# A hybrid S5/conformer decoder layer: the S5 scan by round, the out-projection by token tile, joint evacuation of two tiles

## The chip, the cores and the metric

The kernel runs on one core of one Trainium2 chip. The metric is device time in microseconds (us) of one execution, lower is better. Before the change the median of three runs is 2294.46 us (2292.49 to 2294.57).

## What is computed

One inference step of one layer, all in float32: 2048 prompt tokens and 8 further sequences with one token each, model width 1024. Two sub-layers stand one behind the other, each between two RMS norms:

```
h = rmsnorm(x);  p = h @ w_in                       # 1024 -> 512 (u) + 512 (cv) + 512 (cg)
s = S5(u): 32 groups x 64 complex states, a linear recurrence over the tokens;
    y = Re(C h_t) + D u;  a = gelu(y);  s = a * sigmoid(a @ w_glu + b)
c = silu(layernorm(causal depthwise conv, width 31, of cv * sigmoid(cg)))
x = x + rmsnorm(concat(s, c) @ w_out)               # 1024 -> 1024
h = rmsnorm(x);  up = conv3(h @ w_up)               # 1024 -> 2 x 2816
x = x + rmsnorm((silu(up_gate) * up_val) @ w_down)  # 2816 -> 1024
```

The states of the recurrence and of both convolutions are outputs too.

## The kernel before, in words

**Tiles and rounds.** The tokens are cut into six tiles of 344 (the last: 328 and the 8 single tokens), with channels on the partitions (`TILES`, line 24). Two tiles are a round (`ROUNDS`), and `ORDER` (line 32) lists the stages: in(0), in(1), in(2) up to the u columns, out(0), the rest of in(2), ffn(0), out(1), the last down-projection of round 0 as ffn(0,1), ffn(1,0), out(2), ffn(1,1), ffn(2). "in" is the projection by w_in, "out" the GLU and the projection by w_out (`mix_out`, line 2007), "ffn" the up- and down-projections (line 2071).

**Matmuls.** Each operand in float32 is split into a high and a low float32r part, and `group` (line 1105) makes three matmuls for each block of 128 channels: 24 for a 1024-deep product of one tile.

**Weights.** `wl` lists the weight tiles in order of use; each holds up to 128x8x128 values. At its first use a tile is loaded raw (0.52 MB), split by ACT (wh) and VectorE (wlo), and both halves are stored to DRAM (wd); later uses load the two halves, 1.05 MB. There are three raw buffers and three for each half (`NRAW, NW`), and `w_next` (line 872) loads two to three tiles ahead. All these transfers are issued by SyncE (SP).

**PSUM.** The projections rotate through four one-bank tiles `ps` (`ps_tile`, line 613), and results of evacuation through four SBUF buffers of 344 columns (`ev`, line 883).

**S5.** Tokens are cut into chunks of 8. `s5_part` (line 1471) loads u and the matrix Bd into the slot UR (and ST), multiplies, scans over the chunks on VectorE with a doubling scheme (`fma`, levels `lev`), stores the last state (CR), multiplies by Md and Cd and stores the result (ad); `s5_out` (line 1609) loads it back and applies the GELU. Scans are made for round 0 (86 chunks, two parts of 16 groups) and for rounds 1 and 2 together (170 chunks, four parts of 8 groups).

**Convolution.** `conv(r)` (line 1676) runs 31 taps over four channel blocks and two halves on VectorE, then the layer norm. For rounds 1 and 2 the result is stored (cd) and loaded again by `fetch` (cf); `split_c` (line 1768) makes cHL for the out-projection.

**Background work.** S5, conv, the norms after a projection (`mid`, line 1798: RMS norm, residual x from DRAM as xr, store x1d, second norm) and `finish` are generators. They are spawned with a due number, and advanced between matmul groups as long as estimated engine clocks (`clk`) allow. `back(r)` (line 2164) spawns conv(r) and the S5 parts at the start of ffn(r-1).

**Order.** A `Recorder` collects all instructions. `place()` (line 253) simulates the engines with cost formulas, takes among the ready instructions the one with the lowest priority number, and so fixes the order of every engine's queue and the buffer of every tile. `first(n)` (line 202) lowers the number by n. An instruction goes to the chip by one line, L408, so the profile tells the groups apart by tile names.

```
SCANS = [(0,), (1, 2)]
ps_mm = pool("ps_mm", NPS, space=bass.MemoryType.PSUM)      # NPS = 4
for m in range(8):                                          # out-projection
    w_ = w_next()
    for i in ROUNDS[r]:
        ps = ps_tile()
```

Of the kernel before, what the change touches and what calls it, by code (L numbers as in the profile page):

```python
# [19 lines left out]
G = 32  # L20
# [5 lines left out]
CHUNKS = [86, 86, 84]  # L26
SCANS = [(0,), (1, 2)]
S5_LOAD = [2500, 5000]
S5_TURN = [7500, 9000]
PARTS = [4, 4, 4, 4, 6]  # L30
# [5 lines left out]
NPS = 4  # L36
EVM = 4
NRAW, NW = 3, 3
PACE = [1.0, 1.6, 1.6]
# [492 lines left out]
def kernel(  # L532
# [80 lines left out]
    def ps_tile():  # L613
        if len(out_at) >= NPS:
            wait_pe(out_at[-NPS])
        return ps_mm.tile([128, 512], F32, name="ps", tag="mm")

# [88 lines left out]
    def free(n=1):  # L706
        live[0] -= n
# [14 lines left out]
    msk = const.tile([128, 16], F32, name="msk")  # L722
    mi = small.tile([128, 16], I32, name="mi", tag="ev", bufs=EVM)
    nc.gpsimd.iota(mi, pattern=[[1, 16]], base=112, channel_multiplier=-1)
# [20 lines left out]
    h0 = const.tile([128, 2, 16, NS], F32, name="h0")  # L745
    CR = [const.tile([128, 2, 16], F32, name=f"CR{j}") for j in range(2)]
    aS = const.tile([128, 4, NS], F32, name="aS")
# [49 lines left out]
    for what in ORDER:  # L797
        if what[0] == "in":
            for o in IN_ORDER[what[2]:what[3]]:
                wl.append(cols(w_in, 0, 8, o * 128, 128))  # L800
        elif what[0] == "out":
            for o in range(2):
                wl.append(cols(w_glu, 0, 4, o * 256, 256))
            for o in range(8):
                wl.append(cols(w_out, 0, 8, o * 128, 128))
        else:
            for kind, a in ffn_steps[what[1]][what[2]]:
                if kind == "up":
                    wl.append(cols(w_up, 0, 8, a * 128, 128))
                    wl.append(cols(w_up, 0, 8, (NJ + a) * 128, 128))  # L810
                else:
                    for m in range(16 if what[1:] == (2, 1) else 8):
                        m %= 8
                        wl.append(cols(w_down, part_of[a][0], part_of[a][-1] + 1, m * 128, 128))
# [20 lines left out]
    def w_load_to(i):  # L835
        while w_pos[0] <= min(i, len(wl) - 1):
            n = w_pos[0]
            src, sh, key = wl[n]
            if first_use[key] != n:
                hl = halves[n] = w_tiles(n)  # L840
                for k in range(2):
                    nc.sync.dma_start(hl[k].bitcast(F32), staged[first_use[key]][:, k])
                w_pos[0] += 1
                continue
            t = wp.tile([128, 8, 128], F32, name="wraw", tag="raw", bufs=NRAW)
            v = t.rearrange("p a b -> p (a b)")[:, :sh[0] * sh[1]].rearrange("p (a b) -> p a b", a=sh[0])
            nc.sync.dma_start(v, src)
            w_raw[n] = v
            w_pos[0] += 1

    def w_split_to(i):
        while w_pos[1] <= min(i, len(wl) - 1):
            n = w_pos[1]
            if n in halves:
                hl = w_shaped(n, halves.pop(n))
            else:
                raw = w_raw.pop(n)
                flat = w_tiles(n)
                hl = w_shaped(n, flat)
                with nc.first(700 if n > 1 else 0):  # L860
                    act(hl[0], raw)
                    m = hl[0].shape[1] // 2
                    for c in (slice(0, m), slice(m, 2 * m)):
                        tt(hl[1][:, c], raw[:, c], hl[0][:, c].bitcast(F32), OP.subtract)
                if n in staged:
                    for k in range(2):
                        nc.sync.dma_start(staged[n][:, k], flat[k].bitcast(F32))
            w_hl[n] = hl
            w_at[n] = max(clk.values())
            w_pos[1] += 1  # L870
# [12 lines left out]
    def ev(name, shape=None):  # L883

        return view(small.tile([128, EV], F32, name=name, tag="ev", bufs=EVM), shape or [128, EV])

    def bev(name, shape=None):

        return view(small.tile([128, EV], F32, name=name, tag="bev", bufs=8 - EVM), shape or [128, EV])

# [15 lines left out]
    scans = [0]  # L906
    S5_PARTS = [[(0, g) for g in range(0, G, 16)], [(1, g) for g in range(0, G, 8)]]

# [562 lines left out]
    def s5_part(j, g0, ng):  # L1471

        C = sum(CHUNKS[r] for r in SCANS[j])
        last = j == 1
        C8 = C + (NS if last else 0)
        gp = 2 if last else 4
        na = ng // 2
        yield both(flag("mats"), *(flag("u", r) for r in SCANS[j]))
        if last:
            yield flag("carry", 0, g0 // 16 * 16)  # L1480
        if g0 >= 2 * ng:
# [61 lines left out]
        scans[0] += 1  # L1543
        if last:
            fma(R[:, :, :, 0:1], CR[0][:, :, ha].unsqueeze(3), PWr[:, 0, :, ha], PWi[:, 0, :, ha], 1)
            yield None
# [17 lines left out]
        for n in range(2):  # L1564
            for b in range(2):
                o = S[n * 64:(n + 1) * 64, b::2]
                i = slice(b * 64, (b + 1) * 64)
                copy(o[:, :, 1:C], R[i, n, :, 0:C - 1], "act")
                if last:
                    copy(o[:, :, 0], CR[0][i, n, ha], "act")  # L1570
                    copy(o[:, :, C:C8], h0[i, n, ha], "act")
                else:
                    nc.vector.memset(o[:, :, 0], 0.0)
            yield None
# [34 lines left out]
    def s5_out(r):  # L1609

        C = CHUNKS[r]
        last = r == 2
        j = min(r, 1)
        yield both(*(flag("y", *k) for k in S5_PARTS[j]))
        yield can(1)
        t = slot([128, 4, 8, C], F32, f"aR{r}")
        c0 = sum(CHUNKS[SCANS[j][0]:r])
        src = add[j].rearrange("g h t c -> (g h) t c").rearrange("(k p) t c -> p k t c", p=128)
        for k in range(4):
            nc.sync.dma_start(t[:, k], src[:, k, :, c0:c0 + C])  # L1620
        if last:
            nc.sync.dma_start(aS, ads.rearrange("g h c -> (g h) c").rearrange("(k p) c -> p k c", p=128))
        yield after(0)
        tf = t.rearrange("p k t c -> p (k t c)")
        act(tf, tf, AF.Gelu)
        if last:
            act(aS, aS, AF.Gelu)
        aR[r] = t
        flags["a", r] = True
# [46 lines left out]
    def conv(r):  # L1676
# [6 lines left out]
        if r:  # L1683
            yield both(*(flag("y", *k) for k in S5_PARTS[1][:2]))
        yield can(1)
# [182 lines left out]
    def finish_end(i, y, sqs):  # L1868
# [10 lines left out]
        for c in range(3):  # L1879
            xt = XT[c // 2][:m, c % 2]  # L1880
            for b in range(2):
                if n > 3 and n < 6:
                    yt = ps_tr.tile([128, 512], F32, name="trp", tag="tr")
                else:
                    yt = ps_mm.tile([128, 512], F32, name="ps", tag="mm")
                for k in range(4):
# [16 lines left out]
    def out_ssm():  # L1903
        yield both(*(flag("carry", *k) for k in S5_PARTS[1]))
        yield after(6000)
        t, = yield from raw_tiles(1)
        pt = yield from tr_tile()
        for n in range(2):
            tr(pt[:16, n * 128:n * 128 + 128], CR[1][:, n], ident)
            tr(pt[:, 256 + n * 128:384 + n * 128], hS[:, n].rearrange("p s a -> p (s a)"), ident)  # L1910
# [42 lines left out]
    def mix_in(r, x0, x1):  # L1953
# [17 lines left out]
        for oi, n in seq:  # L1971
# [10 lines left out]
            if oi < 4:  # L1982
                us = ev("us", [128, 8, 43])
                act(us[:, :, :cn].rearrange("p s c -> p c s"), ps[:, :np_].rearrange("p (c s) -> p c s", s=8))
                if w > np_:
                    act(uS[:, oi, :], ps[:, np_:w])
                c0 = n * 43 + (CHUNKS[1] if r == 2 else 0)
                nc.sync.dma_start(udd[min(r, 1)][oi * 128:(oi + 1) * 128, :, c0:c0 + cn], us[:, :, :cn])
            elif oi < 8:
# [17 lines left out]
    def mix_out(r):  # L2007
# [37 lines left out]
        for i in ROUNDS[r]:  # L2045
            sqs[i] = small.tile([128, 344], F32, name="msq", tag="msq", bufs=2)
        for m in range(8):
            w_ = w_next()
            for i in ROUNDS[r]:
                w = wid(i)  # L2050
# [7 lines left out]
                tick()  # L2058
        free(4)
        for i in ROUNDS[r]:  # L2060
            spawn(mid(i, mx[i], sqs[i]), 375 + 400 * r)
# [9 lines left out]
    def ffn(r, last):  # L2071
# [9 lines left out]
        for kind, a in ffn_steps[r][last]:  # L2081
            if kind == "up":
# [9 lines left out]
                for hv in range(2):  # L2092
                    w_ = w_next()
                    jj = hv * NJ + j
                    for n, i in enumerate(ROUNDS[r]):
                        t0, np_, ns = TILES[i]
# [4 lines left out]
                              lambda k: hl[1][:, k, 0:w + 2], 8)  # L2101
                        acc = ev("acc")
                        act(acc[:, :w], ps[:, 2:w + 2], AF.Identity, scale=FC[:, jj, 2:3], bias=FC[:, jj, 3:4])
# [60 lines left out]
    def back(r):  # L2164
        spawn(conv(r), 260 + 400 * r, ("dve", "act"), PACE[r])
        if r < 2:
            for n, (j, g0) in enumerate(S5_PARTS[r]):
                spawn(s5_part(j, g0, G // len(S5_PARTS[r])), 190 + n + 400 * r, pace=PACE[r])
        if r == 0:
            spawn(s5_out(r), 192)  # L2170
# [70 lines left out]
```

## Time and profile before

| | |
|---|---|
| median of the runs | 2294.46 us |
| profiled execution | 2296.11 us |
| its span | 2294.3 us |
| TensorE busy | 2186.8 us (95%) |
| VectorE busy | 1540.8 us (67%) |
| ScalarE busy | 867.9 us (38%) |
| GpSimd busy | 103.8 us (5%) |
| DMA | 436.32 MB, mean 190 GB/s |
| mean granted TensorE clock | 0.969 of full speed |

The span runs from the first to the last instruction. PE is TensorE's matmul, PEld its weight load, DVE VectorE, ACT ScalarE, POOL GpSimd, SP SyncE. The granted clock is a share of 2.4 GHz; 0.5 is 1.2 GHz. A group reads "out<-in": the tile written and those read. The DMA share is the mean busy share of the 16 DMA engines, so 1.0 means that all were busy all the time. A wait is put down to the engine and tile that came last.

### The profile page before, as it was taken

The numbers are of one execution on the slowest core, as the hardware profiler recorded it, in microseconds if no ns is written. First come the engines' busy times: TensorE is split into PE (matmuls) and PEld (weight loads), VectorE is DVE, ScalarE is ACT, GpSimd is POOL, SyncE is SP. The second block draws the span as 40 slices with busy tenths as digits, with TensorE's granted clock in tenths as the row PEclk, the third lists the DMA queues.
The fourth block names the chain that finished last, engine by engine and source line by source line (L and its number), as shares of the span: only waits on it lengthen the run. The fifth ranks groups of instructions, "written<-read, shape, count | busy, mean of one in ns | idle before, by whom it ended". The sixth has DMA issues, their size and how long they took to land.

```text
span 2294.3 us, 36725 instructions
## 1 busy us (share of the span) xinstructions
PE 2186.8 (95%) x13923; PEld 2169.6 (95%) x13923; DVE 1540.8 (67%) x3636; ACT 867.9 (38%) x1677; POOL 103.8 (5%) x114
## 2 busy tenths in 40 slices
PE   8998889999999999986899999999998999999998
PEld 8998889999998999976899999999998999999998
DVE  7979865379698999961799995544428624334344
ACT  5665345345543534432443212243225322112134
POOL 1465000000000000000000000000000000000000
PEclk9998789999999999997999999999999999999999
DMA  9999857695858576544654443463546543443546
GB/s 303 273 303 263 193 160 239 165 287 171 256 177 249 165 247 215 179 154 166 218 204 150 157 142 116 153 193 133 193 148 214 178 140 118 165 133 125 186 160 215
DMA packets 267549, 436.32 MB, mean 190 GB/s; under 512 B 60736, under 2 KB 165944, under 8 KB 263733
## 3 DMA queue, kind: packets, MB, share of 16 engines
q1 hardware_dynamic: 266630, 432.62, 59.7%
q8 instruction: 110, 1.80, 0.3%
q0 software_dynamic: 352, 0.67, 0.1%
q10 hardware_dynamic: 391, 0.69, 0.1%
q14 instruction: 66, 0.54, 0.1%
HBM read 293.02 MB, written 140.37 MB: 189 GB/s over the span
## 4 chain that ended last, share of the span: by engine, by line
PE 84%; DVE 9%; DMA 3%; ACT 2%; issue 1%; SPq 1%; POOL 0%; DVEq 0%; ACTq 0%; POOLq 0%
PE ps L408 79%; PE trp L408 4%; DVE acc L408 3%; DVE ST L408 1%; DVE UR L408 1%; DVE wlo L408 1%; DVE mx L408 1%; DMA UR<-ud 1%; DVE st L408 1%; DMA xa<-in_x_prompt_dram 1%; SPq L408 1%; DVE sqs L408 1%; DMA ST<-Bd 0%; ACT UR L408 0%; DVE c L408 0%
## 5 line engine op out<-in xcount | busy, mean ns | idle before, releaser
L408 PE MATMUL ps<-h,wh 128*128 128x346 f32 (+3 forms) x5376 | 1295.2, 323 | 16.1 <-ACT us L408 7.7
L408 PEld LDWEIGHTS ps<-h,wh 128*128 128x128 f32 x5376 | 937.6, 190 | 18.1 <-ACT us L408 7.8
L408 PE MATMUL ps<-h,wlo 128*128 128x346 f32 (+3 forms) x2688 | 866.2, 322 | 0.4 <-DMA wlo<-wd 0.4
L408 PE MATMUL ps<-f,wh 128*128 128x344 f32 (+1 forms) x2112 | 503.6, 322 | 8.8 <-DVE y L408 8.8
L408 PEld LDWEIGHTS ps<-h,wlo 128*128 128x128 f32 x2688 | 510.0, 190 | 0.8 <-DMA wlo<-wd 0.7
L408 DVE SCALAR_TENSOR_TENSOR acc<-ps,FC,acc 128x344 f32<-128x344 f32 (+1 forms) x528 | 302.1, 573 | 266.9 <-ACT acc L408 191.7
L408 PEld LDWEIGHTS ps<-f,wh 128*128 128x128 f32 x2112 | 366.1, 189 | 9.2 <-DVE y L408 9.0
L408 DVE SCALAR_TENSOR_TENSOR acc<-c,V,acc 128x344 f32<-128x344 f32 (+1 forms) x609 | 350.3, 575 | 10.6
L408 PE MATMUL ps<-f,wlo 128*128 128x344 f32 (+1 forms) x1056 | 338.9, 321 | 0.0
L408 ACT ACTIVATE acc<-ps,FC 128x344 f32<-128x344 f32 (+1 forms) x264 | 167.5, 635 | 367.1 <-PE ps L408 366.2
L408 PEld LDWEIGHTS ps<-f,wlo 128*128 128x128 f32 x1056 | 199.6, 189 | 0.0
L408 DVE TENSOR_TENSOR y<-y,ps 128x344 f32<-128x344 f32 (+1 forms) x192 | 97.1, 508 | 115.1 <-PE ps L408 114.8
L408 DVE TENSOR_TENSOR wlo<-wraw,wh 128x512 fp32r<-128x512 f32 (+2 forms) x212 | 122.6, 620 | 45.2 <-ACT wh L408 44.5
L408 ACT ACTIVATE f<-acc 128x344 fp32r<-128x344 f32 (+1 forms) x132 | 64.8, 491 | 224.1 <-DVE acc L408 223.8
L408 ACT ACTIVATE wh<-wraw 128x1024 fp32r<-128x1024 f32 (+2 forms) x106 | 96.5, 912 | 94.5 <-PE ps L408 66.4
L408 ACT ACTIVATE acc<-acc 128x344 f32<-128x344 f32 (+1 forms) x132 | 64.8, 491 | 171.3 <-DVE acc L408 169.8
L408 DVE TENSOR_TENSOR msq<-msq,sq 128x344 f32<-128x344 f32 (+1 forms) x84 | 42.9, 514 | 115.2 <-ACT sq L408 115.1
L408 PE MATMUL ps<-cHL,wh 128*128 128x344 f32 (+1 forms) x384 | 94.2, 328 | 18.5 <-ACT cHL L408 18.1
L408 PE MATMUL ps<-sHL,wh 128*128 128x344 f32 (+1 forms) x384 | 92.7, 324 | 0.0
L408 DVE TENSOR_TENSOR f<-acc,f 128x344 fp32r<-128x344 f32 (+1 forms) x132 | 67.8, 514 | 36.0 <-ACT f L408 35.3
L408 POOL TENSOR_TENSOR cacc<-cacc,wk 128x344 f32<-128x344 f32 x87 | 87.1, 1002 | 87.4 <-ACT wk L408 82.7
L408 PEld LDWEIGHTS ps<-cHL,wh 128*128 128x128 f32 x384 | 68.6, 195 | 19.7 <-ACT cHL L408 18.7
(230 smaller groups left out, 2035.9 us busy)
## 6 DMA issues: line engine op xcount, KB each, us to landing
wh<-wd SPq DMA_DIRECT2D x132, 512.0 KB
wlo<-wd SPq DMA_DIRECT2D x132, 512.0 KB
wd<-wh SPq DMA_DIRECT2D x66, 512.0 KB
wd<-wlo SPq DMA_DIRECT2D x66, 512.0 KB
wraw<-in_w_up_dram SPq DMA_DIRECT2D x44, 512.0 KB
wh<-wd SPq DMA_DIRECT2D x64, 256.0 KB
wlo<-wd SPq DMA_DIRECT2D x64, 256.0 KB
wh<-wd SPq DMA_DIRECT2D x24, 384.0 KB
```

The source lines that it names most:

```text
L408: o.call(*[real(a) for a in o.args], **{k: real(a) for k, a in o.kw.items()})
```

## The change

- The S5 scan is made for each round by itself: three scans of 86, 86 and 84 chunks, each in two parts of 16 groups, with the carry of the round before (CR). Round 2's parts are spawned with conv(2), at the start of ffn(1,0). conv(1) and conv(2) wait for the first part of their own round.
- In the out-projection the loop over tiles is outside, the loop over the eight w_out tiles inside. So w_out is listed twice for each out stage, and `mid` of the first tile is spawned after its eight groups.
- PSUM is allocated as two pairs of banks. In the up-projections of rounds 0 and 1 both tiles of the round are computed into one pair and evacuated by one instruction each (ACT, two VectorE multiply-adds, SiLU or product, split). All other users take the halves of a pair one after the other. The ev buffers become three pairs of 2 x 344.
- Weight loads get a priority number lower by 700, the stores of halves one higher by 400; there are two raw buffers.

```diff
-SCANS = [(0,), (1, 2)]
-S5_LOAD = [2500, 5000]
-S5_TURN = [7500, 9000]
+SCANS = [(0,), (1,), (2,)]
+S5_LOAD = [2500, 5000, 5000]
+S5_TURN = [7500, 7500, 7500]
-EVM = 4
-NRAW, NW = 3, 3
+EVM = 3
+NRAW, NW = 2, 3
 def ps_tile():
         if len(out_at) >= NPS:
             wait_pe(out_at[-NPS])
-        return ps_mm.tile([128, 512], F32, name="ps", tag="mm")
+        if not half:
+            t = ps_mm.tile([128, 2, 512], F32, name="ps", tag="mm", bufs=NPS // 2)
+            half.append(t[:, 1])
+            return t[:, 0]
+        return half.pop()
+    def ps_pair():
+        half.clear()
+        if len(out_at) >= NPS // 2:
+            wait_pe(out_at[-(NPS // 2)])
+        return ps_mm.tile([128, 2, 512], F32, name="ps", tag="mm", bufs=NPS // 2)
...
-            for o in range(8):
-                wl.append(cols(w_out, 0, 8, o * 128, 128))
+            for o in range(16):
+                wl.append(cols(w_out, 0, 8, o % 8 * 128, 128))
...
-                for k in range(2):
-                    nc.sync.dma_start(hl[k].bitcast(F32), staged[first_use[key]][:, k])
+                with nc.first(700):
+                    for k in range(2):
+                        nc.sync.dma_start(hl[k].bitcast(F32), staged[first_use[key]][:, k])
-            nc.sync.dma_start(v, src)
+            with nc.first(700 if n > 1 else 0):
+                nc.sync.dma_start(v, src)
-                    for k in range(2):
-                        nc.sync.dma_start(staged[n][:, k], flat[k].bitcast(F32))
+                    with nc.first(-400):
+                        for k in range(2):
+                            nc.sync.dma_start(staged[n][:, k], flat[k].bitcast(F32))
 def ev(name, shape=None):
-        return view(small.tile([128, EV], F32, name=name, tag="ev", bufs=EVM), shape or [128, EV])
+        if not spare_ev:
+            t = ev2(name)
+            spare_ev.append(t[:, 1])
+            return view(t[:, 0], shape or [128, EV])
+        return view(spare_ev.pop(), shape or [128, EV])
+    def ev2(name):
+        return small.tile([128, 2, EV], F32, name=name, tag="ev", bufs=EVM)
...
-    S5_PARTS = [[(0, g) for g in range(0, G, 16)], [(1, g) for g in range(0, G, 8)]]
+    S5_PARTS = [[(j, g) for g in range(0, G, 16)] for j in range(3)]
 def s5_part(j, g0, ng):
-        last = j == 1
+        last = j == 2
-        gp = 2 if last else 4
+        gp = 4
-        if last:
-            yield flag("carry", 0, g0 // 16 * 16)
+        if j:
+            yield flag("carry", j - 1, g0)
...
 def conv(r):
         if r:
-            yield both(*(flag("y", *k) for k in S5_PARTS[1][:2]))
+            yield both(*(flag("y", *k) for k in S5_PARTS[r][:1]))
 def mix_out(r):
-        for m in range(8):
-            w_ = w_next()
-            for i in ROUNDS[r]:
+        for i in ROUNDS[r]:
+            for m in range(8):
+                w_ = w_next()
...
-        free(4)
-        for i in ROUNDS[r]:
+            free(2)
             spawn(mid(i, mx[i], sqs[i]), 375 + 400 * r)
 def ffn(r, last):
+                    if r < 2:
+                        w = wid(ROUNDS[r][0])
+                        ps = ps_pair()
+                        for n, i in enumerate(ROUNDS[r]):
+                            hl = hT[i]
+                            group(ps[:, n, :w + 2], w_, slice(0, 128), lambda k: hl[0][:, k, 0:w + 2],
+                                  lambda k: hl[1][:, k, 0:w + 2], 8)
+                        acc = ev2("acc")
+                        act(acc, ps[:, :, 2:w + 2], AF.Identity, scale=FC[:, jj, 2:3], bias=FC[:, jj, 3:4])
+                        stt(acc, ps[:, :, 1:w + 1], FC[:, jj, 1:2], acc, OP.mult, OP.add)
+                        stt(acc, ps[:, :, 0:w], FC[:, jj, 0:1], acc, OP.mult, OP.add)
+                        if hv == 0:
+                            act(acc, acc, AF.Silu)
+                            gs = acc
+                        else:
+                            tt(acc, acc, gs, OP.mult)
+                            fv = [ft[:, sub, x].rearrange("p (n c) -> p n c", n=2) for x in range(2)]
+                            act(fv[0], acc)
+                            tt(fv[1], acc, fv[0].bitcast(F32), OP.subtract)
+                        tick()
+                        continue
...
 def back(r):
-        if r < 2:
-            for n, (j, g0) in enumerate(S5_PARTS[r]):
-                spawn(s5_part(j, g0, G // len(S5_PARTS[r])), 190 + n + 400 * r, pace=PACE[r])
+        for n, (j, g0) in enumerate(S5_PARTS[r]):
+            spawn(s5_part(j, g0, G // len(S5_PARTS[r])), 190 + n + 400 * r, pace=PACE[r])
```

## Rows read from the trace of the kernel before

**Rows 1.** Page, busy time: engine, us, share of the span, instructions

```profile
PE 2186.8 (95%) x13923; PEld 2169.6 (95%) x13923; DVE 1540.8 (67%) x3636; ACT 867.9 (38%) x1677; POOL 103.8 (5%) x114
```

**Rows 2.** Waits of TensorE, whole span: engine, waited for, us, times, longest

```profile
PE ps L408 <- ACT cHL L408: 18.1, 2, 16.5
PE ps L408 <- DVE y L408: 8.8, 2, 4.7
PE trp L408 <- DVE Rs L408: 3.0, 4, 1.4
PE trp L408 <- ACT ys L408: 2.3, 2, 1.8
PE ps L408 <- DMA wlo<-wd: 0.4, 1, 0.4
```

**Rows 3.** 50 us stretches: length, PE, PEld, DVE, ACT, POOL busy, PEclk, DMA share, GB/s

```profile
200.00:250.00 50.00, 47.05 (x265) 46.38 (x265) 46.58 (x130) 18.46 (x42) 12.94 (x12) 0.84 0.99 202
900.00:950.00 50.00, 50.00 (x315) 50.00 (x315) 49.22 (x98) 20.52 (x34) 0.00 (x0) 1.00 0.58 190
1000.00:1050.00 50.00, 23.37 (x142) 21.31 (x140) 23.45 (x51) 16.69 (x32) 0.00 (x0) 0.71 0.28 99
1100.00:1150.00 50.00, 40.78 (x265) 40.34 (x264) 43.25 (x133) 26.01 (x52) 0.00 (x0) 0.90 0.68 240
1400.00:1450.00 50.00, 50.00 (x319) 49.92 (x318) 24.05 (x47) 11.14 (x20) 0.00 (x0) 1.00 0.34 109
1700.00:1750.00 50.00, 43.34 (x288) 42.68 (x287) 39.02 (x121) 22.82 (x49) 0.00 (x0) 0.93 0.58 207
```

**Rows 4.** The same table in 10 us stretches, around out(1) and out(2)

```profile
1050.00:1060.00 10.00, 9.17 (x43) 8.76 (x44) 3.24 (x4) 5.46 (x10) 0.00 (x0) 0.72 0.48 163
1060.00:1070.00 10.00, 10.00 (x66) 10.00 (x65) 2.08 (x4) 2.69 (x7) 0.00 (x0) 1.00 0.59 200
1130.00:1140.00 10.00, 7.11 (x36) 7.11 (x37) 9.76 (x33) 5.92 (x12) 0.00 (x0) 0.63 0.73 276
1730.00:1740.00 10.00, 5.62 (x28) 5.61 (x29) 9.86 (x31) 6.08 (x13) 0.00 (x0) 0.66 0.61 220
```

**Rows 5.** Chain that ended last: start us, us, what

```profile
231.49 11.18 DMA UR<-ud
1034.83 1.60 DVE c L408
1038.86 5.30 DMA cd<-c
1044.17 5.81 DMA cf<-cd
```

**Rows 6.** Instructions on tile UR alone, 480 to 800: sum and mean

```profile
sum 320.00, PE 31.75 PEld 26.64 DVE 94.25 ACT 32.05 POOL 0.46; mean PE 1.98 PEld 1.67 DVE 5.89 ACT 2.00 POOL 0.03
```

**Rows 7.** Groups by line: out<-in, form, count, busy us, mean ns, idle before

```profile
L408 DVE SCALAR_TENSOR_TENSOR mx<-mx,V,sqs 128x344 f32<-128x344 f32 (+1 forms) x48 | 24.6, 570 | 0.0
L408 DVE TENSOR_TENSOR mx<-mx,msq 128x344 f32<-128x344 f32 (+1 forms) x48 | 22.9, 506 | 10.5 <-ACT msq L408 10.5
L408 DVE TENSOR_TENSOR h<-mx,h 128x688 fp32r<-128x688 f32 (+1 forms) x24 | 19.5, 868 | 0.0
```

**Rows 8.** Timeline of TensorE, S5 matmuls: start us, us, what, count

```profile
200.88 7.13 PE L408 MATMUL trp<-UR,ST 128*128 128x86 f32 x32
560.61 1.37 PE L408 MATMUL trp<-UR,ST 128*128 128x178 f32 x8
```

**Rows 9.** The table again, two stretches with heavy DMA

```profile
620.00:640.00 20.00, 18.59 (x118) 18.34 (x117) 15.27 (x43) 10.38 (x24) 0.00 (x0) 1.00 1.01 335
2240.00:2270.00 30.00, 30.00 (x204) 29.94 (x203) 11.16 (x31) 12.42 (x25) 0.00 (x0) 1.00 0.84 276
```

**Rows 10.** Tiles cd and cHL: count, ns min/median/max, first and last start us

```profile
L408 SPq DMA_DIRECT2D cd<-c x2: 555/557/559, 1038.9 to 1512.2; - x2
L408 ACT ACTIVATE cHL<-cf x8: 755/762/782, 1050.0 to 1650.2; 128x688 fp32r<-128x688 f32 x6, 128x672 fp32r<-128x672 f32 x2
```

More of the change, by code (lines that the diff above doesn't have):

```diff
@@ L615, in ps_tile @@
             wait_pe(out_at[-NPS])
-        return ps_mm.tile([128, 512], F32, name="ps", tag="mm")
+        if not half:
[3 more added lines that the diff above has]
+        return half.pop()
+    half = []
+    def ps_pair():
[3 more added lines that the diff above has]
+        return ps_mm.tile([128, 2, 512], F32, name="ps", tag="mm", bufs=NPS // 2)
     tasks = []
@@ L722 @@
     msk = const.tile([128, 16], F32, name="msk")
-    mi = small.tile([128, 16], I32, name="mi", tag="ev", bufs=EVM)
+    mi = const.tile([128, 16], I32, name="mi")
     nc.gpsimd.iota(mi, pattern=[[1, 16]], base=112, channel_multiplier=-1)
@@ L745 @@
     h0 = const.tile([128, 2, 16, NS], F32, name="h0")
-    CR = [const.tile([128, 2, 16], F32, name=f"CR{j}") for j in range(2)]
+    CR = [const.tile([128, 2, 16], F32, name=f"CR{j}") for j in range(3)]
     aS = const.tile([128, 4, NS], F32, name="aS")
@@ L883, in ev @@
     def ev(name, shape=None):
-        return view(small.tile([128, EV], F32, name=name, tag="ev", bufs=EVM), shape or [128, EV])
+        if not spare_ev:
[3 more added lines that the diff above has]
+        return view(spare_ev.pop(), shape or [128, EV])
+    spare_ev = []
+    def ev2(name):
+        return small.tile([128, 2, EV], F32, name=name, tag="ev", bufs=EVM)
     def bev(name, shape=None):
-        return view(small.tile([128, EV], F32, name=name, tag="bev", bufs=8 - EVM), shape or [128, EV])
+        return view(small.tile([128, EV], F32, name=name, tag="bev", bufs=4), shape or [128, EV])
     def tr_tile():
@@ L1543, in s5_part @@
         scans[0] += 1
-        if last:
-            fma(R[:, :, :, 0:1], CR[0][:, :, ha].unsqueeze(3), PWr[:, 0, :, ha], PWi[:, 0, :, ha], 1)
+        if j:
+            fma(R[:, :, :, 0:1], CR[j - 1][:, :, ha].unsqueeze(3), PWr[:, 0, :, ha], PWi[:, 0, :, ha], 1)
             yield None
@@ L1569, in s5_part @@
                 if last:
-                    copy(o[:, :, 0], CR[0][i, n, ha], "act")
                     copy(o[:, :, C:C8], h0[i, n, ha], "act")
+                if j:
+                    copy(o[:, :, 0], CR[j - 1][i, n, ha], "act")
                 else:
@@ L1612, in s5_out @@
         last = r == 2
-        j = min(r, 1)
+        j = r
         yield both(*(flag("y", *k) for k in S5_PARTS[j]))
@@ L1884, in finish_end @@
                 else:
-                    yt = ps_mm.tile([128, 512], F32, name="ps", tag="mm")
+                    yt = ps_tile()
                 for k in range(4):
@@ L1903, in out_ssm @@
     def out_ssm():
-        yield both(*(flag("carry", *k) for k in S5_PARTS[1]))
+        yield both(*(flag("carry", *k) for k in S5_PARTS[2]))
         yield after(6000)
@@ L1908, in out_ssm @@
         for n in range(2):
-            tr(pt[:16, n * 128:n * 128 + 128], CR[1][:, n], ident)
+            tr(pt[:16, n * 128:n * 128 + 128], CR[2][:, n], ident)
             tr(pt[:, 256 + n * 128:384 + n * 128], hS[:, n].rearrange("p s a -> p (s a)"), ident)
@@ L1986, in mix_in @@
                     act(uS[:, oi, :], ps[:, np_:w])
-                c0 = n * 43 + (CHUNKS[1] if r == 2 else 0)
-                nc.sync.dma_start(udd[min(r, 1)][oi * 128:(oi + 1) * 128, :, c0:c0 + cn], us[:, :, :cn])
+                c0 = n * 43
+                nc.sync.dma_start(udd[r][oi * 128:(oi + 1) * 128, :, c0:c0 + cn], us[:, :, :cn])
             elif oi < 8:
@@ L2094, in ffn @@
                     jj = hv * NJ + j
+                    if r < 2:
[19 more added lines that the diff above has]
+                        continue
+                    pair = ev2("acc")
                     for n, i in enumerate(ROUNDS[r]):
@@ L2101, in ffn @@
                               lambda k: hl[1][:, k, 0:w + 2], 8)
-                        acc = ev("acc")
+                        acc = pair[:, n]
                         act(acc[:, :w], ps[:, 2:w + 2], AF.Identity, scale=FC[:, jj, 2:3], bias=FC[:, jj, 3:4])
```

## The prediction, made before the change was run

> **What bounds the kernel now.** I read the page first: TensorE is busy for 95% of the span, VectorE for 67%, ACT for 38% [rows 1]. So the time can fall only where TensorE stands still or runs at its lower clock, or where matmuls go away; no weight matmul goes away here. In steady state TensorE issues 66 matmuls in 10 us, one every 0.152 us, so a group of 24 takes 3.65 us [rows 4].
>
> The list of what TensorE waited for comes next [rows 2]: operands that ACT and VectorE prepare, cHL first, and weights (wlo) hardly at all. The table by 50 us stretches shows where [rows 3]. Behind the start-up there are three holes, each around an out-projection:
>
> - 1000 to 1050: 26.6 us idle [rows 3]. Behind it 43 matmuls take 9.17 us where 6.5 would do, at a granted clock of 0.72, so partly at 1.2 GHz [rows 4]. With the few slow matmuls inside the hole about **30 us**.
> - 1100 to 1150: 9.2 us idle [rows 3], and 36 matmuls in 7.11 us instead of 5.5 [rows 4]: **10.8 us**.
> - 1700 to 1750: 6.7 us idle [rows 3], and 28 matmuls in 5.62 us instead of 4.3 [rows 4]: **8 us**.
>
> The chain of waits names the first hole [rows 5]: the layer norm of conv(1) on VectorE (c), the store cd, the reload cf, and only then out(1). VectorE is full before it, 49.2 of 50 us up to 950 [rows 3]. In the second and third hole VectorE is full too (9.8 of 10 us from 1130 and from 1730 [rows 4]) with mid of both token tiles at once, and a matmul waits for the VectorE add into y that frees its PSUM [rows 2].
>
> **The change part by part.**
>
> *S5 per round.* From 480 to 800 the instructions on the S5 buffer UR keep VectorE for 94.3 us [rows 6], for rounds 1 and 2 together. Half of it, 47 us, moves behind round 1, into ffn(1,0), where VectorE has 26 us in 50 free from 1400 on [rows 3]. conv(1) then waits for one scan part instead of two of the same size. As VectorE is full for most of the stretch before the first hole, conv(1) should end about 47 us earlier.
>
> *Joint evacuation.* With VectorE full, an instruction costs 0.50 us (98 in 49.2 [rows 3]). Between the 344 and the 688 form of a VectorE operation (506 and 868 ns [rows 7]) 344 elements are 0.36 us, so merging two saves 0.14. Each j loses six VectorE instructions (four multiply-adds, one product, one difference); 20 j lie before the hole: 120 x 0.14 = 17 us of VectorE. ACT gains as well and binds nowhere.
>
> Together 64 us less VectorE work against a hole of 27: I take the whole **-30 us**; what is late next is TensorE itself. The other end is 0, if conv(1)'s taps are issued no earlier though VectorE is freer.
>
> *Out-projection tile by tile.* mid of the first tile now starts 8 groups (29 us) earlier, where VectorE is nearly idle (2.1 of 10 us at 1060 [rows 4]). Three groups of mid and split alone are 22.9 + 24.6 + 19.5 us for six tiles [rows 7], 11 us a tile, more than the 9.2 and 6.7 us idle. I take **-9** and **-6.5 us** and keep 0 as the other end, for the second tile's mid still meets the last down-projection.
>
> *What S5 per round costs TensorE.* Rounds 1 and 2 have 32 channel groups x 3 matmuls, each two instructions, of 178 columns: 8 in 1.37 us [rows 8], less the last one's latency 0.15 us each, 29 us in all. Afterwards they are twice as many, of 86 or 92 columns. In proportion to columns one would be 0.074 us (-1 us in all); at an unchanged 0.15, +29. The trace has the 86-column shape at half clock, 32 in 7.13 us [rows 8], 0.216 us each, so 0.108 at full clock: 41 us. That row is nearest: **+12 us**. Of the waits for Rs and ys (3.0 + 2.3 us [rows 2]) those of round 1 go, for only the last round has sample columns: **-2 us**. The third load of Bd, Md and Cd (6.3 MB, with 20 or so issues on SP) lies in ffn(1,0) at a DMA share of 0.34 [rows 3] and costs nothing; with that cover gone it would be 19 us of DMA at 335 GB/s [rows 9].
>
> *What tile by tile costs in DMA.* Every 3.65 us group now needs a weight tile of its own. A reload is 1.05 MB: 287 GB/s. In the first pass of out(0) it is 0.52 MB raw and 1.05 MB stored: 431 GB/s. The trace carries 276 GB/s for 30 us with TensorE full, in the last down-projection, and 335 GB/s for 20 us at a DMA share of 1.01 [rows 9]. The first pass, 12.6 MB, takes 37.6 us at 335 instead of 29.2: +8, up to +16 at 276, and 0 if the stores lag without harm. **+8 us.** By the Trainium skill (DMA: Bandwidth & Descriptors, Specifications) a core's limit at HBM is about 358 GB/s; an estimate from that is 35 us and +6. The trace's 335 at a full share lies just under it.
>
> In out(1) and out(2) the rate is within what the trace carries. What can delay a weight is xr or x1d ahead of it in SP's queue, 1.41 MB or 4.2 us at 335, plus its own 3.1 us, against a lead of two groups, 7.3 us, by three buffers. That just fits; at 276 instead of 287 each stage loses 2.5 us. **+2 us each**, 0 to 8. VectorE and ACT have room for the splits there.
>
> *PSUM and SBUF buffers.* Four single PSUM tiles become two pairs: a tile is free only when its neighbour is evacuated too, so the lead falls from three groups to two. Evacuating a pair (one ACT, two VectorE operations of about 0.9 us) stands against 7.3 us of matmuls: 0, at most the 8.8 us of waits for y [rows 2] once more. Six ev halves for four: 0.
>
> *Order of loads and stores.* Weight loads get ahead, stores fall back, and two raw buffers replace three, all on the SP queue that holds S5's UR loads, 11.2 us of the chain at 231 [rows 5], at a DMA share of 0.99 [rows 3]. Two weight tiles more ahead of them are 6 us, two less give as much; I take 0, with 8 either way.
>
> Sum: -30 - 9 - 6.5 - 2 + 12 + 8 + 4 = -23.5 us. The profiled execution took 2296.1 us (span 2294.3), 1.65 above the median of the runs. 2296.1 - 23.5 = 2272.6, on the median's scale **2271 us**.
>
> **The rivals.**
>
> 1. *The first hole stays.* The order of every queue is planned ahead from costs; if conv(1)'s taps keep their places, only a quarter of the 30 us comes back. For: the hole ends with a store and a reload in series, not with work. Against: VectorE is full up to 950. 2271 + 22 = 2293 us; chance 0.11.
> 2. *Out(2) waits instead.* conv(2) now waits for S5 of its own round. It was stored at 1512 and used by 1650 [rows 10], 138 us later; 47 us of S5 at half of VectorE free delay it by 94. If the delay passes 138 us, it decides, and a hole like the first returns: about 2296 us; chance 0.05.
> 3. *Slower: the out-projections become bound by weight loads.* If the DMA engines carry no more than 276 GB/s, the first pass costs 16 us, the other 42 MB of reloads 6, and xr and x1d, 4.2 MB in each of three stages, 45: 67 us instead of my 12, 2271 + 55 = 2326 us. It turns the change slower from 36 us of such loss on. For: the first pass asks for more than any row carries. Against: 276 runs with TensorE full. Chance 0.13.
> 4. *Pairs starve TensorE of PSUM.* Where VectorE is full, two groups of lead may be too few: 0.3 us for each of 88 pairs is 26 us, 2297 us. Against: four singles are waited for in two places only [rows 2]. The Trainium skill (Perfetto Trace Analysis, Matmuls) wants independent groups to rotate through banks so that one's evacuation overlaps the next's matmuls; two pairs still do that, with less lead. Chance 0.05.
>
> **How the numbers follow.** The forecast has 0.66; its own range is 2252 to 2290 (DMA terms at 0 and at double, start-up 8 either way). With the rivals the range is 2240 to 2301. A measurement of this kernel tells about 0.2% (4.6 us) from no change. Faster: 0.66, half of the first rival and 0.02 of the second: 0.74. Same: the rest of those two and some of the fourth: 0.10. Slower: 0.16.
>
> **What would show each step.** Right: no wait for cHL before out(1), VectorE below 90% in the 150 us ahead of it; no waits for y behind out(1) and out(2); S5 matmuls in two stretches, 384 of 86 or 92 columns at 0.108 us; about 290 GB/s in the out stages with under 12 us of TensorE waits for wh, wlo or their splits. Wrong: waits for weights of more than 36 us, a wait for cHL before out(2), or short regular waits of ps for acc in the up-projections.

## The result, and the profile after

The change made the kernel slower by an eighth: a median of 2577.69 us (2575.96 to 2580.85) beside 2294.11 us (four runs of each), ratio 1.1239 with a 95% interval of 1.1220 to 1.1259, so 283.6 us more. The forecast was 2271, its highest end 2301.

The page, busy times of the changed kernel (span 2574.1 us; to be read against [rows 1]):

```profile
PE 2293.0 (89%) x14115; PEld 2185.7 (85%) x14115; DVE 1519.7 (59%) x3290; ACT 826.1 (32%) x1485; POOL 105.1 (4%) x112
```

TensorE has 192 matmuls more (S5, as forecast), but its idle time grew from 107.5 us (2294.3 - 2186.8) to 281.1 us (2574.1 - 2293.0). That is 174 us. The other 106 us are hidden in "busy". A matmul is recorded for 0.32 us though the next one starts 0.156 us behind it, so at each stop the tail of the last one counts as busy time, and the first one behind a stop is recorded longer (0.42 us in the timeline below). Added up from rows below, it is 0.29 us a stop, 89 us for the 307 short waits; the S5 matmuls are some 14 us more. The weight loads (PEld), which do not grow that way, tell more: 94.6% of the span before, 84.9% after.

What TensorE waited for, whole span of the changed kernel (us in total, times, longest; against [rows 2]):

```profile
PE ps L408 <- DVE acc L408: 62.0, 88, 0.7
PE ps L408 <- DVE y L408: 57.9, 90, 4.6
PE ps L408 <- ACT acc L408: 30.8, 43, 0.7
PE ps L408 <- ACT sq L408: 20.0, 19, 9.1
PE ps L408 <- ACT y L408: 13.3, 24, 0.7
PE ps L408 <- ACT gt L408: 13.2, 22, 1.0
PE ps L408 <- ACT mx L408: 12.9, 21, 0.7
...
PE ps L408 <- ACT cHL L408: 5.2, 1, 5.2
...
PE ps L408 <- DMA wlo<-wd: 0.2, 1, 0.2
```

The seven groups at the top are 307 short waits, nearly all of 0.5 to 0.7 us, and each group is a wait for an instruction that empties PSUM (acc, y, sq, gt, mx). The large single waits are not the news: cHL fell from 18.1 to 5.2 us, all of it before out(0) and none before out(1), as forecast, and weights are hardly waited for.

Stretches of the changed kernel (length, PE, PEld, DVE, ACT, POOL busy, PEclk, DMA share, GB/s; against [rows 3]):

```profile
900.00:950.00 50.00, 50.00 (x316) 49.80 (x315) 28.73 (x38) 18.34 (x23) 0.00 (x0) 1.00 0.62 207
1000.00:1050.00 50.00, 44.52 (x275) 41.95 (x273) 29.42 (x61) 23.42 (x33) 0.00 (x0) 1.00 0.70 242
1400.00:1450.00 50.00, 45.16 (x275) 42.89 (x274) 43.71 (x78) 4.18 (x5) 0.00 (x0) 1.00 0.34 117
1700.00:1750.00 50.00, 43.16 (x257) 40.04 (x257) 25.13 (x44) 18.95 (x34) 0.00 (x0) 1.00 0.59 208
1950.00:2250.00 300.00, 245.63 (x1427) 223.69 (x1426) 79.14 (x165) 53.62 (x116) 0.00 (x0) 0.99 0.29 100
```

The hole at 1000 to 1050 is gone, and VectorE has room ahead of it (28.73 of 50 us; it was full). But 300 us of ffn(2) now hold 1427 matmuls, at a granted clock of 0.99 and with VectorE at a quarter. The same stretch of the kernel before has 1924, one every 0.156 us:

```profile
1950.00:2250.00 300.00, 300.00 (x1924) 299.75 (x1923) 115.85 (x240) 68.79 (x146) 0.00 (x0) 1.00 0.47 158
```

The joint up-projections of ffn(0) run at the old rate (900 to 950); ffn(2), which still evacuates singly, does not. Its chain of waits repeats every 10.45 us (start us, us, what; the first repetition, and the first row of the next two):

```profile
2050.16 0.65 ACT acc L408
...
2050.85 0.89 PE ps L408 x4
...
2051.83 0.59 DVE acc L408
...
2052.46 0.89 PE ps L408 x4
...
2053.38 0.58 DVE acc L408
...
2054.01 6.57 PE ps L408 x40
...
2060.60 0.65 ACT acc L408
...
2071.06 0.65 ACT acc L408
```

One repetition is one pair of 24-matmul groups, 48 x 0.156 = 7.48 us before. So 2.97 us are lost per pair. The 48 matmuls themselves take 6.57 + 0.89 + 0.89 = 8.35 us of the chain, 0.87 more for three stops. The timeline of one pair (start us, us, what, idle before it and its releaser; the first half has been filled up to 2060.25, matmuls of 338 columns go into the second half):

```profile
2060.09 0.47 PE L408 MATMUL ps<-h,wh 128*128 128x338 f32 x2
2060.60 0.64 ACT L408 ACTIVATE acc<-ps,FC 128x344 f32<-128x344 f32 x1 [1.63 <-PE ps L408]
...
2061.29 0.43 PE L408 MATMUL ps<-h,wlo 128*128 128x338 f32 x1 [0.73 <-ACT acc L408]
...
2062.27 0.57 DVE L408 SCALAR_TENSOR_TENSOR acc<-ps,FC,acc 128x344 f32<-128x344 f32 x1 [3.89 <-PE ps L408]
...
2062.90 0.57 PE L408 MATMUL ps<-h,wh 128*128 128x338 f32 x2 [0.74 <-DVE acc L408]
...
2063.82 0.58 DVE L408 SCALAR_TENSOR_TENSOR acc<-ps,FC,acc 128x344 f32<-128x344 f32 x1 [0.97 <-PE ps L408]
...
2064.45 0.42 PE L408 MATMUL ps<-h,wh 128*128 128x338 f32 x1 [0.67 <-DVE acc L408]
```

The first two matmuls into the second half pass. Then ACT reads the *first* half, not at 2060.25 when that is full but behind those two; the third matmul, which writes the *second* half, waits until ACT is done. Four matmuls later VectorE reads the first half and waits for those four, and the next matmul waits for VectorE; once more for its second instruction. TensorE and the evacuating engines take turns three times per pair, once for each instruction that empties the first half.

**Theory, "shared tile":** the two halves of a pair are one tile; whatever stands behind an access to one half in the planned order waits for it, though it touches the other half. The planner does not see it: `Recorder.add` compares the ranges of columns (`box`), finds no overlap, and places the evacuation in the middle of the next group. **Rivals:** "less lead" (a pair comes free only when both halves are out, so PSUM runs short; the fourth rival of the prediction) and "another part" of the change.

### The profile page after: what moved, and what is told of

It reads as the page before. It is cut to its first block, busy times and chain, and to the rows that moved or that the text cites. A ratio compares the mean times of both kernels' runs of the same rounds, so it can differ in the third digit from the quotient of the medians.

```text
span 2574.1 us, 36490 instructions
## 1 busy us (share of the span) xinstructions
PE 2293.0 (89%) x14115; PEld 2185.7 (85%) x14115; DVE 1519.7 (59%) x3290; ACT 826.1 (32%) x1485; POOL 105.1 (4%) x112
## 4 chain that ended last, share of the span: by engine, by line
PE 80%; DVE 11%; ACT 5%; DMA 2%; issue 2%; SPq 0%; DVEq 0%; ACTq 0%
PE ps L408 76%; PE trp L408 4%; DVE acc L408 4%; DVE y L408 2%; ACT acc L408 1%; DVE mx L408 1%; DMA xb<-in_x_prompt_dram 1%; DVE UR L408 1%; DVE ST L408 1%; ACT UR L408 0%; ACT mx L408 0%; ACT y L408 0%; ACT gt L408 0%; DVE w L408 0%; DVE h L408 0%
## 5 line engine op out<-in xcount | busy, mean ns | idle before, releaser
L408 PE MATMUL ps<-h,wh 128*128 128x346 f32 (+3 forms) x5376 | 1318.7, 327 | 84.5 <-DVE acc L408 57.7
L408 PE MATMUL ps<-h,wlo 128*128 128x346 f32 (+3 forms) x2688 | 875.6, 326 | 44.8 <-ACT acc L408 30.6
L408 PE MATMUL ps<-f,wh 128*128 128x344 f32 (+1 forms) x2112 | 512.6, 324 | 31.9 <-DVE y L408 21.6
L408 DVE SCALAR_TENSOR_TENSOR acc<-ps,FC,acc 128x688 f32<-128x688 f32 (+2 forms) x352 | 263.6, 749 | 391.6 <-PE ps L408 218.1
L408 PE MATMUL ps<-f,wlo 128*128 128x344 f32 (+1 forms) x1056 | 348.4, 330 | 48.4 <-DVE y L408 36.3
L408 ACT ACTIVATE acc<-ps,FC 128x688 f32<-128x688 f32 (+2 forms) x176 | 136.6, 776 | 477.7 <-PE ps L408 474.0
L408 ACT ACTIVATE f<-acc 128x688 fp32r<-128x688 f32 (+1 forms) x88 | 55.7, 633 | 235.5 <-DVE acc L408 235.4
L408 ACT ACTIVATE acc<-acc 128x688 f32<-128x688 f32 (+1 forms) x88 | 55.7, 633 | 185.3 <-DVE acc L408 183.9
L408 PE MATMUL ps<-sHL,wh 128*128 128x344 f32 (+1 forms) x384 | 94.6, 329 | 3.5 <-ACT mx L408 2.0
L408 PE MATMUL ps<-sHL,wlo 128*128 128x344 f32 (+1 forms) x192 | 66.7, 347 | 23.5 <-ACT mx L408 10.8
L408 DVE TENSOR_TENSOR f<-acc,f 128x688 fp32r<-128x688 f32 (+1 forms) x88 | 60.9, 692 | 32.2 <-ACT f L408 32.2
```

The source lines that it names most:

```text
L408: o.call(*[real(a) for a in o.args], **{k: real(a) for k, a in o.kw.items()})
```

## The experiments

Each ratio is to the kernel before as measured again beside that run (medians of 2296 to 2298 us). Microseconds worked out from a ratio are the ratio times 2294.

**1 and 2. On the kernel before: halves alone, whole pairs alone.** Nothing else of the change is in these two. Both have two tiles of two banks in rotation; the first hands out both halves, the second only the first half of each (its planner is told of a lead of two). The transposes of `finish` take their tile from `ps_tile` as well.

```diff
 e3_halves
-        return ps_mm.tile([128, 512], F32, name="ps", tag="mm")
+        if not half:
+            t = ps_mm.tile([128, 2, 512], F32, name="ps", tag="mm", bufs=NPS // 2)
+            half.append(t[:, 1])
+            return t[:, 0]
+        return half.pop()
 l1_lead
-        return ps_mm.tile([128, 512], F32, name="ps", tag="mm")
+        t = ps_mm.tile([128, 2, 512], F32, name="ps", tag="mm", bufs=NPS // 2)
+        return t[:, 0]
```

Expected of the halves:

> The kernel before with one thing changed: single PSUM tiles are handed out as the two halves of a pair, as in the changed kernel; everything is still evacuated singly. 'Shared tile': every up-projection now has the waits that the changed kernel has in ffn(2) only, so more than its whole loss of 283 us: 2600 to 2850 us, and TensorE waits for acc all over the span. 'Less lead': slower as well, but with one wait per pair, at its first matmul. 'Another part': 2294 us.

Expected of the whole pairs:

> The kernel before with one thing changed: every single group gets a whole pair of banks (two tiles in rotation instead of four), nothing shared and nothing evacuated jointly. Beside the run with halves (2885 us, same two pairs) it separates the two theories on the same kernel. 'Shared tile': what is left here is the shorter rotation alone, 10 to 40 us by the runs of the changed kernel (2315 against 2279 us): 2306 to 2336 us. 'Less lead': about the halves' time, over 2600 us.

Measured: halves 2884.69 us, ratio 1.2553 (1.2520 to 1.2587); whole pairs 2326.98 us, 1.0128 (1.0104 to 1.0151). TensorE's waits with halves:

```profile
PE ps L408 <- DVE acc L408: 178.6, 253, 1.5
PE ps L408 <- ACT acc L408: 97.0, 128, 2.2
PE ps L408 <- DVE y L408: 60.4, 85, 4.2
```

and with whole pairs:

```profile
PE ps L408 <- DVE acc L408: 17.5, 27, 2.6
...
PE ps L408 <- DVE y L408: 15.3, 10, 4.2
```

With the same number of tiles in rotation, sharing alone costs 586 - 29 = 557 us. "Less lead" is real, but it is the 29 us. The halves went past the expected range because I scaled too low. Up-projections have 44 pairs a round, 132 in all, and 381 waits for acc are 2.9 for each; in the changed kernel the 131 waits for acc are 3.0 for each of the 44 pairs of ffn(2). 132 x 2.97 = 392 us, and the other waits of this kind come on top, as does a lower clock: its mean is 0.953, beside 0.969 before.

**3. On the changed kernel: another order of the same halves.**

```diff
 e4_alternate
-            t = ps_mm.tile([128, 2, 512], F32, name="ps", tag="mm", bufs=NPS // 2)
-            half.append(t[:, 1])
-            return t[:, 0]
+            t = [ps_mm.tile([128, 2, 512], F32, name="ps", tag="mm", bufs=NPS // 2) for _ in range(2)]
+            half.extend([t[1][:, 1], t[0][:, 1], t[1][:, 0]])
+            return t[0][:, 0]
```

> The changed kernel with one thing else: single groups still get halves of two-bank tiles, but in the order first half of one pair, first half of the other, second half of the first, second half of the other. 'Shared tile': the evacuation of the neighbouring half then lies a whole group (3.65 us) behind and is done when the matmuls reach it, so the waits for acc in the last 600 us fall from 89 to below 15 us and the time is about that of the whole pairs (2315 us), 2285 to 2340. If two neighbouring banks disturb one another in use, or halves as such are slow (rival): no change, 2560 us or more.

Measured: 2305.48 us, ratio 1.0031 (1.0019 to 1.0043), so 277 us came back by the order in which the same halves are handed out. No wait for acc is left in the last 600 us. The stretch that held 1427 matmuls:

```profile
1950.00:2250.00 300.00, 299.93 (x1910) 298.93 (x1910) 116.95 (x243) 65.65 (x142) 0.00 (x0) 1.00 0.46 155
```

This order keeps the two halves of one pair a whole group apart, so it does not by itself test neighbouring banks in use together. The durations do: emptying 344 columns takes ACT 635 ns in the kernel before (220 times), beside running matmuls, and 637 ns in the changed kernel's ffn(2) (44 times), where TensorE stands still for it; VectorE takes 576 ns in both. So these rows show no sign of one bank disturbing another. The Trainium skill (PSUM — Partial Sum Buffer, PSUM bank collisions raise a hardware error) names the bank, within a quadrant of partitions, as what accesses must be kept apart in, with different banks in use together. By that rule the halves needed no wait at all, and the kernel before, whose four one-bank tiles are filled and emptied by turns at 1924 matmuls in 300 us, agrees. The waits are for semaphores of the program, from which the profile infers who released whom: they belong to the program's order, not to the memory.

**4. On the changed kernel: whole pairs for single groups.** The joint evacuation stays.

```diff
 e1_whole
-        if not half:
-            t = ps_mm.tile([128, 2, 512], F32, name="ps", tag="mm", bufs=NPS // 2)
-            half.append(t[:, 1])
-            return t[:, 0]
-        return half.pop()
+        t = ps_mm.tile([128, 2, 512], F32, name="ps", tag="mm", bufs=NPS // 2)
+        return t[:, 0]
```

> The changed kernel, but every single group gets a whole pair of banks and uses its first half; the joint evacuation of the pairs stays. Theory 'shared tile' (the matmuls of a group that stand behind the evacuation of the pair's other half wait for it): no group shares a tile any more, so the waits of ps for acc, 91 us in 1900 to 2500, fall below 10 us and the time comes to 2265 to 2300 us. Theory 'less lead' (a pair comes free only when both halves are out, so TensorE runs out of PSUM): single groups now rotate through two tiles only, less than in the changed kernel, so the waits stay or grow and the time is 2570 us or more. Theory 'another part' (tile by tile, S5 per round or the order of loads holds TensorE up): 2540 us or more, whatever the waits for acc do.

Measured: 2315.05 us, ratio 1.0077 (1.0058 to 1.0095): 267 us better. The waits of the whole span:

```profile
PE ps L408 <- DVE y L408: 28.4, 7, 12.9
...
PE ps L408 <- DVE acc L408: 3.3, 6, 1.6
```

The waits for acc are gone. The time stands 15 us above my range: I had taken the shorter rotation as free once more. What it does shows in y, 25 of the 28.4 us lie behind out(1) and out(2), where VectorE is busy with mid.

**5. On the changed kernel: the buffers of before.** Four single PSUM tiles, four single ev tiles, no joint evacuation; all else of the change stays.

```diff
 e2_singles
-EVM = 3
+EVM = 4
-        if not half:
...
+        return ps_mm.tile([128, 512], F32, name="ps", tag="mm")
...
-                    if r < 2:
-                        w = wid(ROUNDS[r][0])
-                        ps = ps_pair()
...
-                        acc = pair[:, n]
+                        acc = ev("acc")
```

> The changed kernel with the buffers of the kernel before (four single PSUM tiles, four single ev tiles, no joint evacuation); S5 per round, the out-projection tile by tile, the order of loads and two raw buffers stay. 'Shared tile' and 'less lead' both: 2265 to 2300 us, by the terms of the prediction 2275. 'Another part': 2540 us or more.

Measured: 2279.03 us, ratio 0.9919 (0.9892 to 0.9946), 19 us faster than before. So the rest of the change does gain, and the buffers alone turn the sign: 1.1239 - 0.9919 = 0.132, 303 us.

**6. Joint evacuation,** with whole pairs for single groups, and with the ev halves and two raw buffers of the change.

```diff
 p4_joint
-EVM = 4
-NRAW, NW = 3, 3
+EVM = 3
+NRAW, NW = 2, 3
...
+        t = ps_mm.tile([128, 2, 512], F32, name="ps", tag="mm", bufs=NPS // 2)
+        return t[:, 0]
...
+                    if r < 2:
+                        w = wid(ROUNDS[r][0])
+                        ps = ps_pair()
...
```

> The kernel before with the joint evacuation and its pairs, two raw buffers, and whole pairs for single groups; S5 in two scans, the out-projection and the order of loads as before. By the prediction's step 17 us of VectorE work leave the time ahead of the first hole: 2275 to 2294 us under 'shared tile'; under 'less lead' 2400 us or more.

Measured: 2318.82 us, ratio 1.0094 (1.0078 to 1.0111), above the expected range. Against the whole pairs alone (1.0128) that is some 8 us better, but the intervals overlap, and the ev halves with two raw buffers are as much faster by themselves (experiment 10). So a gain of joint evacuation is not shown; it does not pay for the two tiles that it takes from the rotation. Nor does the first hole shrink, which had a wait of 16.5 us for cHL before:

```profile
PE ps L408 <- ACT cHL L408: 19.9, 2, 16.8
```

**7. S5 per round alone** (`SCANS`, `S5_LOAD`, `S5_TURN`, a third CR, the flags and `back` as in the change).

```diff
 p1_s5
-SCANS = [(0,), (1, 2)]
+SCANS = [(0,), (1,), (2,)]
...
-        if r < 2:
-            for n, (j, g0) in enumerate(S5_PARTS[r]):
-                spawn(s5_part(j, g0, G // len(S5_PARTS[r])), 190 + n + 400 * r, pace=PACE[r])
+        for n, (j, g0) in enumerate(S5_PARTS[r]):
+            spawn(s5_part(j, g0, G // len(S5_PARTS[r])), 190 + n + 400 * r, pace=PACE[r])
```

> The kernel before with S5 per round and nothing else. By the prediction's terms: -30 (conv(1) earlier; 47 us of VectorE leave it), -2, +12 (S5 matmuls): 2276 us, and the hole at 1000 to 1050 gone. By the rival 'the first hole stays': 2294 to 2310 us with a wait for cHL of 16 us.

Measured: 2266.85 us, ratio 0.9862 (0.9844 to 0.9880), 32 us faster. Two stretches of it:

```profile
500.00:850.00 350.00, 349.87 (x2261) 349.43 (x2260) 333.26 (x714) 140.46 (x253) 0.00 (x0) 1.00 0.69 222
1000.00:1050.00 50.00, 50.00 (x324) 49.99 (x323) 9.92 (x21) 14.15 (x31) 0.00 (x0) 1.00 0.49 165
```

the first of them in the kernel before:

```profile
500.00:850.00 350.00, 337.03 (x2105) 333.54 (x2104) 314.78 (x823) 156.55 (x328) 0.31 (x2) 1.00 0.69 214
```

and S5 matmuls in its timeline of TensorE:

```profile
562.36 0.39 PE L408 MATMUL trp<-UR,ST 128*128 128x86 f32 x2
...
565.04 0.39 PE L408 MATMUL trp<-UR 128*128 128x86 f32 x2
```

The hole is gone: 26.6 us of idle time [rows 3], with the slow matmuls behind it. The stretch of the two-round scan loses 12.8 us of idle time (12.97 to 0.13), which I had at 2 us. Between these two rows 24 S5 matmuls start in 2.68 us, 0.112 each where I took 0.108: 384 x 0.112 - 29 = +14 us.

**8. The out-projection tile by tile alone.**

```diff
 p2_tbt
-            for o in range(8):
-                wl.append(cols(w_out, 0, 8, o * 128, 128))
+            for o in range(16):
+                wl.append(cols(w_out, 0, 8, o % 8 * 128, 128))
...
-        for m in range(8):
-            w_ = w_next()
-            for i in ROUNDS[r]:
+        for i in ROUNDS[r]:
+            for m in range(8):
+                w_ = w_next()
...
```

> The kernel before with the out-projection tile by tile and nothing else. By the prediction's terms: -9 - 6.5 + 8 + 4 = -3.5: 2292 us; by the rival 'bound by weight loads' 2350 us.

Measured: 2308.98 us, ratio 1.0049 (1.0032 to 1.0065), 11 us slower. TensorE's waits:

```profile
PE ps L408 <- DMA wh<-wd: 9.7, 3, 4.3
PE ps L408 <- ACT sq L408: 8.3, 1, 8.3
...
PE ps L408 <- DMA wlo<-wd: 5.3, 9, 1.1
...
PE ps L408 <- DVE y L408: 3.7, 1, 3.7
```

The weights cost 15 us of waits where before they cost 0.4 [rows 2]. For y 3.7 us are waited instead of 8.8, but one wait for sq of 8.3 us is new: behind out(1) the hole only changed its place.

**9. The order of loads and stores alone** (weight loads first, stores later, two raw buffers).

```diff
 p3_order
-NRAW, NW = 3, 3
+NRAW, NW = 2, 3
...
+                with nc.first(700):
...
+            with nc.first(700 if n > 1 else 0):
...
+                    with nc.first(-400):
...
```

> The kernel before with the order of weight loads and stores and two raw buffers, and nothing else. By the prediction 0, 8 us either way: 2288 to 2304 us.

Measured: 2295.84 us, ratio 0.9992 (0.9981 to 1.0002): no difference.

**10. The halves in SBUF alone.**

```diff
 v1_ev
-EVM = 4
-NRAW, NW = 3, 3
+EVM = 3
+NRAW, NW = 2, 3
...
-        return view(small.tile([128, EV], F32, name=name, tag="ev", bufs=EVM), shape or [128, EV])
+        if not spare_ev:
+            t = ev2(name)
+            spare_ev.append(t[:, 1])
+            return view(t[:, 0], shape or [128, EV])
+        return view(spare_ev.pop(), shape or [128, EV])
```

> The kernel before with one thing changed: the SBUF tiles ev (gt, vt, us, acc, s2, sq) are handed out as halves of three two-row tiles instead of four singles (and two raw buffers, which makes the room). 'Shared tile' holds for SBUF too, but only ACT and VectorE stand in it, which have room: 2290 to 2320 us. If SBUF halves carry a part of the loss: over 2340 us.

Measured: 2289.39 us, ratio 0.9966 (0.9951 to 0.9981), 8 us faster. The SBUF halves carry nothing of the loss. Why the run is faster, with six halves for four singles, stays open.

**11 and 12. Versions that beat both kernels.** S5 per round with the order of loads, then S5 per round with the SBUF halves; each is the sum of two diffs above.

```diff
 b1_s5order, b2_s5ev
-SCANS = [(0,), (1, 2)]
+SCANS = [(0,), (1,), (2,)]
...
```

> The kernel before with S5 per round and the order of loads and stores (two raw buffers), and nothing else of the change. From the single runs: 2267 - 2 = 2265 us (2258 to 2272); it beats both kernels if the parts add up.

Measured: 2270.30 us, ratio 0.9882 (0.9859 to 0.9904).

> The kernel before with S5 per round and the SBUF ev tiles as halves (two raw buffers), PSUM as before, out-projection and order of loads as before. If the two single results add up (-1.38% and -0.34%): 2258 us (2250 to 2264). If the gain of the ev halves was a chance effect of another planned order: 2266 to 2275 us, the time of S5 per round alone.

Measured: 2260.91 us, ratio 0.9851 (0.9833 to 0.9870). It has the lowest median, but its interval overlaps that of S5 per round alone (0.9844 to 0.9880), so that is what can be claimed: S5 per round gains 1.4%, and neither addition to it can be told from nothing.

## Why the prediction was wrong

**The step that failed is "PSUM and SBUF buffers",** costed at 0, at most 8.8 us. It asked when a pair comes *free* ("a tile is free only when its neighbour is evacuated too") and set that against 7.3 us of matmuls. It did not ask what happens between the halves while one is being read and the other written. In its place the runs showed 303 us from the buffers of the changed kernel, of which 267 came back with whole pairs instead, or 277 with another order of the halves: the shared tile.

The trace's numbers add up to it. Up-projections of ffn(2): 44 pairs x 2.97 = 131 us. Waits for y: 114 [the list of waits above], each with a restart; the chain of the changed kernel has a down-projection pair of 24 matmuls every 4.66 us:

```profile
1031.67 0.52 DVE y L408
...
1032.23 4.07 PE ps L408 x24
...
1036.33 0.53 DVE y L408
```

Against 24 x 0.156 = 3.74 that is 0.92 us each, 105 us. The other waits for gt, mx and sq are 62; an estimate at the same price is 57 us. Together 293 us, against 267 to 277 given back and 303 for the buffers as a whole. (The prediction's 0.152 us a matmul is a count in 10 us; over 300 us it is 0.156, which makes its DMA rates for the out stages some 2.5% too high.)

**The fourth rival** had the right place and the wrong mechanism. Its 26 us for two groups of lead are close to the 29 us (24 to 35) of the whole pairs, but by luck: 0.3 us for each of 88 pairs was a guess, and the run shows 27 waits for acc and 10 for y, 33 us in all. I gave it 0.05, against rows in which four singles are waited for in two places only [rows 2]. The whole list has two more waits for an instruction that empties PSUM (into the tile `us`, 7.7 us; into `gt`, 1.0 us), and none of these rows says anything about two pairs. The Trainium skill (Perfetto Trace Analysis, Matmuls) wants independent groups in different banks so that evacuation and matmuls overlap; I wrote that two pairs still do that. The banks were different, but in the planned order the groups were no longer independent, and the timeline above shows no overlap. The one sign that I named for it, short regular waits of ps for acc, is what came.

**S5 per round:** right, and larger than forecast, -32 us for -20. The hole went as the chain of waits said [rows 5], and conv(1) met a VectorE with room. The +12 for the matmuls measured +14 (the half-clock row was the right one to scale). Mis-sized was the -2 for waits in the two-round scan, 12.8 us of idle time there. -30 - 12.8 + 14 makes -29; the other 3 us are not pinned down.

**Out-projection tile by tile:** wrong sign, +11 us for -3.5. Its DMA term was about right (+12; 15 us of waits for weights). What failed are the -9 and -6.5. They took the holes for waits for y alone, but in the second 5.1 of the 9.2 us are a wait of the transposes for sqs, the sums of squares in mid (kernel before, 1080 to 1180). I had kept 0 as the other end, "for the second tile's mid still meets the last down-projection", and with 15 us of new waits for weights and +11 us in all, or +6 in the profiled execution (2302.09 us, the fastest of eight), only some 4 to 9 us of gain are left. The third rival, a bound by weight loads at 2326 us, did not come.

**Joint evacuation:** the -17 us of VectorE work were to end conv(1) earlier, but with joint evacuation and without S5 per round the wait for cHL stays (16.8 us beside 16.5); S5 per round closes that hole alone. A gain of its own is not shown, and its pairs cost 29.

**Order of loads and stores:** right, 0. The single parts add up too: -32 + 11 - 2 = -23 us, against -19 (-25 to -12) for all three together.

## What to carry to other kernels

Before two independent pieces of work are put into one allocated tile, ask what orders accesses to that tile: if it is the tile and not the range, a reader of one half stops the writer of the other, and the planner's own test of overlap may not know it. If a large tile must be shared, hand out its parts so that neighbours are a whole group apart in time; here that is worth 277 us and three lines. And a change of several parts is measured part by part: here one part hid a gain of 1.4% behind a loss of 13%.

## What the runs showed of the hardware that was not expected

The busy share of TensorE hid about a third of the loss: 106 of 280 us of additional span were counted as busy, some 14 of them for the additional S5 matmuls. Matmuls per stretch (1924 against 1427 in 300 us) and the weight loads' busy time showed it at once.

Interrupting TensorE three times in 10 us for 0.7 us each hardly lowered its granted clock in the changed kernel: 0.99 in 1950 to 2250, and 1.00 in the other stretches shown. With halves alone it fell more often, 0.97 in 1950 to 2250. In 2265 to 2270 that run has 0.50 (1.2 GHz), straight behind three such waits of 0.73, 0.74 and 0.67 us with TensorE busy for 2.86 of 5 us; at 2270.7, in a row of matmuls without a wait, it is back at 2.4 GHz. Why the same waits lower it in one place and not in another, no run shows.
